# A Mamba-2 and MLA trunk on one core: sums of squares of weights drawn beneath the next projections, stores of converted pairs held back by one load, the first scan in two parts

## Chip, core and metric

The kernel runs on one core of a Trainium2 chip. Its time is the device time of one execution in microseconds (us). A core has a matrix engine (TensorE, PE in the profile), a vector engine (VectorE, DVE), a scalar engine (ScalarE, ACT) and GpSimd (POOL); all of the loads and stores that matter here are issued by SyncE (SP) in one queue. Each engine works through its own instructions in order and waits for others by semaphores.

## The reference

Two layers over 2048 tokens of width 1024, float32. The change lies in the first, a Mamba-2 mixer:

```python
proj = h @ w_in                                  # 1024 -> z 2048, xBC 2048 + 2*4*128, dt 32
z, xBC, dt_raw = jnp.split(proj, [D_INNER, D_INNER + CONV_DIM], axis=-1)
xBC = jax.nn.silu(causal_depthwise_conv(xBC, conv_w, conv_b))
xs, Bm, Cm = jnp.split(xBC, [D_INNER, D_INNER + SSM_GROUPS * SSM_STATE], axis=-1)
dt = jax.nn.softplus((dt_raw + dt_bias).astype(jnp.float32))
y = ssd_chunked_scan(xh, dt, A, Bm, Cm)          # 4 groups of 8 heads of 64, state 128
y = (y + D_skip[:, None] * xh).reshape(Bsz, S, D_INNER) * jax.nn.silu(z)
y = y * lax.rsqrt(jnp.mean(y * y, axis=-1, keepdims=True) + EPS)   # by group
return (y * g_out) @ w_out                       # 2048 -> 1024
```

The second layer is multi-head latent attention (16 heads, 2048 tokens, causal), with a down-projected query and a shared latent key and value, and a final RMS norm follows.

## The kernel before

**Arithmetic.** A float32 product is made of three half-precision ones: each operand is split into a high and a low part (fp16 pairs, or fp32r halves), and `mm3` (L84 to L88) issues high by high, high by low and low by high into one PSUM bank. A weight that is split into an fp16 pair (`pair16`, L117 on ScalarE for the high part, L118 on VectorE for the low one) is first scaled by a power of two, so that its values lie in the range of fp16. That power comes from the weight's sum of squares: `scan` (L164) loads a group's weights tile by tile (L175), squares them on ScalarE with an accumulated sum (L180), adds the sums on VectorE (L183, L185), and `powers` (L140) sums over the partitions with a small matmul (L144) and makes the two powers, `up` and `down`, with eight small VectorE operations.

**Tiling.** The tokens go in 4 blocks of 512 (index b), the channels of the Mamba layer in 4 groups (g). One item is one (b, g). An item's work has four parts:

- `xbc` and `zgate` (L476, L509): the input projections of a group, 24 steps. The weights have three kinds: 0 is the columns of B and C (256 wide), 1 those of x (512), 2 those of the gate z (512). They come from `wpair` (L193). In block 0 it loads raw weights (L206, 3 buffers `wraw`), converts two k-slices into a `wsp` buffer (6 of them) and stores the pair to DRAM (`wi_d`, L209); in later blocks the pair is just loaded back (L211). The evacuations of xbc do the convolution (L494 to L503), those of zgate the gate (`sz`, L523, L524).
- `ssd` (L629): the chunked scan over the item's 512 tokens, cut into 20 pieces. It loads a broadcast of the cumulated decays (`big`, L662, from `cumT`), makes products of B and C (L665, L666), transposes x (L681), and runs a chain over VectorE, ScalarE, GpSimd and PE (L674 to L676, L684, L688, L696, L697, halves at L645 and L646, L702, L713, L718, L720, L723).
- `outp` (L530): the output projection of the item before, 8 steps; in block 0 its weights are loaded, split and stored too (L130, L109 to L113, `wo_d` at L551).
- At some items extra parts: for (0,0) and (0,1) the scan of group g + 2 (11 steps), for (1,0) `head_scale` (L407, 22 steps: 21 pieces of the later weights are loaded, L420, and squared, L421), for g = 2 the loading, normalizing and steps of the next block.

**The order of the work.** `mamba` (L313) makes one item after the other. For item n it lines up the parts: outp of item n − 1, xbc and zgate of item n + 1, then the extra ones. It counts their steps (`total`) and, while it goes through them one after the other, draws a piece of the item's own ssd each time that `done * total < 20 * step`. So the pieces are spread evenly over all the steps, the extra ones too. A scheduler then orders each engine's instructions by program order, as they become possible, with weight loads and their conversions moved ahead by `AHEAD` = 10. In front of the items stand the scan of group 0 by kinds (kind 0 by itself, then 1 and 2 together, the tiles kept in `held` so that they need no second load), `prep` (the norm and the transposes of the first tokens), `steps` (dt and its cumulated sums, L573 and L613 to L625), xbc and zgate of (0,0), and beside both of these the scan of group 1.

## Time and profile before

| | |
|---|---|
| median of 3 runs | 3186.62 us (3184.37 to 3187.11) |
| the profiled execution | 3185.83 us |
| its span in the trace | 3184.1 us |
| its mean granted clock of PE | 0.993 |
| PE busy | 3059.6 us, 96% of the span |
| VectorE, ScalarE busy | 2394.7 us (75%), 1929.9 us (61%) |
| DMA | 454.75 MB, mean 143 GB/s |

Busy time is the time during which an engine has an instruction under way. Stretches of the span are quoted as start:end, length, then the busy time and number of instructions of each engine in the stretch, the granted PE clock, the share of time in which the DMA engines were busy, and GB/s. A row of waits names who waited for what, for how long in total, how often, and the longest. A row of the timeline has the start in us, the length, and at the end in brackets how long the engine stood idle before it and for whom.

### The profile page before, as it was taken

The numbers are of one execution on the slowest core, as the hardware profiler recorded it, in microseconds if no ns is written. First come the engines' busy times: TensorE is split into PE (matmuls) and PEld (weight loads), VectorE is DVE, ScalarE is ACT, GpSimd is POOL, SyncE is SP. The second block draws the span as 40 slices with busy tenths as digits, with TensorE's granted clock in tenths as the row PEclk, the third lists the DMA queues.
The fourth block names the chain that finished last, engine by engine and source line by source line (L and its number), as shares of the span: only waits on it lengthen the run. The fifth ranks groups of instructions, "written<-read, shape, count | busy, mean of one in ns | idle before, by whom it ended". The sixth has DMA issues, their size and how long they took to land.

```text
span 3184.1 us, 51344 instructions
## 1 busy us (share of the span) xinstructions
PE 3059.6 (96%) x17746; PEld 2046.3 (64%) x17746; DVE 2394.7 (75%) x5191; ACT 1929.9 (61%) x4859; POOL 610.5 (19%) x842
## 2 busy tenths in 40 slices
PE   6999999899999999999999999999999999999998
PEld 3455555566556666655788888866666666666677
DVE  7778885677776776776967766668888888888665
ACT  8667554554544444455646554568888888888522
POOL 0212121121222111221211211222212222222100
PEclk9999999999999999999999999999999999999999
DMA  8667645433354344433565555632222322233484
GB/s 289 227 214 229 228 146 195 156 126 127 132 180 133 120 147 153 146 133 108 173 216 185 187 163 171 189 90 51 61 54 55 66 52 65 53 73 88 104 273 157
DMA packets 196586, 454.75 MB, mean 143 GB/s; under 512 B 29107, under 2 KB 52403, under 8 KB 194885
## 3 DMA queue, kind: packets, MB, share of 16 engines
q1 hardware_dynamic: 168468, 373.58, 36.0%
q0 software_dynamic: 27856, 77.89, 9.5%
q8 instruction: 140, 2.29, 0.3%
q14 instruction: 122, 0.99, 0.1%
HBM read 340.60 MB, written 110.76 MB: 142 GB/s over the span
## 4 chain that ended last, share of the span: by engine, by line
PE 64%; DVE 13%; ACT 8%; DMA 6%; issue 6%; POOL 1%; SPq 1%; ACTq 0%; DVEq 0%; POOLq 0%
PE mm L86 13%; PE mm L87 12%; PE mm L88 12%; PE tr L1081 6%; PE tr L87 4%; PE tr L86 4%; PE tr L88 3%; PE tr L1092 3%; PE tr L1091 3%; DVE cacc L500 3%; ACT Pr L1066 2%; DMA big<-cumT 2%; DMA wraw<-in_ssm_w_in_dram 1%; DVE PTs L118 1%; DVE big L674 1%
## 5 line engine op out<-in xcount | busy, mean ns | idle before, releaser
L118 DVE SCALAR_TENSOR_TENSOR PTs<-tr,PTs 128x512 f16<-128x512 f32 (+3 forms) x640 | 373.9, 605 | 77.0 <-ACT PTs L117 69.9
L1066 ACT ACTIVATE Pr<-mm,nm 128x512 f32<-128x512 f32 (+2 forms) x631 | 394.1, 635 | 49.3 <-DVE nm L1058 44.8
L1054 DVE TENSOR_REDUCE mx<-mm 128x1 f32<-128x512 f32 (+2 forms) x631 | 372.6, 602 | 32.4 <-PE mm L88 29.6
L117 ACT ACTIVATE PTs<-tr 128x512 f16<-128x512 f32 (+3 forms) x640 | 329.3, 544 | 99.5 <-PE tr L1081 97.6
L1081 PE MATMUL tr<-pack,Pr 128*128 128x128 f32 x2176 | 317.4, 273 | 1.8 <-ACT Os L1098 1.4
L86 PE MATMUL mm<-xT,wsp 128*128 128x512 f16 (+1 forms) x800 | 304.7, 381 | 0.1
L88 PE MATMUL mm<-xT,wsp 128*128 128x512 f16 (+1 forms) x800 | 303.3, 380 | 1.3 <-DVE wsp L118 1.2
L87 PE MATMUL mm<-xT,wsp 128*128 128x512 f16 (+1 forms) x800 | 303.7, 380 | 0.0
L1081 PEld LDWEIGHTS tr<-pack,Pr 128*128 128x128 f32 x2176 | 253.2, 141 | 69.1 <-ACT Os L1098 2.2
L688 ACT ACTIVATE Xw<-tr,d_wend 128x64 f32<-128x64 f32 x512 | 183.0, 358 | 133.8 <-DVE Xd L684 132.3
L86 PE MATMUL mm<-K,xT 96*128 96x512 f16 (+2 forms) x639 | 222.8, 349 | 27.2 <-ACT Pr L1066 23.7
L500 DVE SCALAR_TENSOR_TENSOR cacc<-craw,pack,cacc 128x512 f32<-128x512 f32 x288 | 213.3, 763 | 29.6 <-ACT cacc L498 28.0
L86 PE MATMUL mm<-wsp,xT 128*128 128x512 f16 (+1 forms) x640 | 232.5, 363 | 1.8 <-ACT craw L494 1.6
L87 PE MATMUL mm<-wsp,xT 128*128 128x512 f16 (+1 forms) x640 | 231.8, 362 | 0.0
L88 PE MATMUL mm<-wsp,xT 128*128 128x512 f16 (+1 forms) x640 | 231.2, 362 | 0.0
L88 PE MATMUL mm<-K,xT 96*128 96x512 f16 (+2 forms) x639 | 222.5, 348 | 0.0
L87 PE MATMUL mm<-K,xT 96*128 96x512 f16 (+2 forms) x639 | 221.7, 347 | 0.0
L1091 PE MATMUL tr<-PTs,xT 128*128 128x512 f16 (+3 forms) x640 | 221.3, 347 | 0.1
L86 PE MATMUL mm<-wsp,yT 128*128 128x512 f32 x512 | 208.4, 410 | 11.9 <-DVE sz L524 6.3
L646 POOL TENSOR_TENSOR Xp<-Xw,Xp 128x512 fp32r<-128x512 f32 x64 | 81.8, 1278 | 717.7 <-ACT Xp L645 389.6
L1092 PE MATMUL tr<-PTs,xT 128*128 128x512 f16 (+3 forms) x640 | 219.4, 347 | 0.0
L87 PEld LDWEIGHTS <-xT 96*128 96x128 f16 (+1 forms) x1152 | 112.7, 98 | 153.7 <-issue 65.0
(431 smaller groups left out, 7341.8 us busy)
## 6 DMA issues: line engine op xcount, KB each, us to landing
wsp<-wi_d SPq DMA_DIRECT2D x96, 512.0 KB, 3.7
wsp<-wo_d SPq DMA_DIRECT2D x96, 512.0 KB, 3.4
big<-cumT SPq DMA_DIRECT2D x64, 512.0 KB, 4.9
wi_d<-wsp SPq DMA_DIRECT2D x32, 512.0 KB, 3.5
wo_d<-wsp SPq DMA_DIRECT2D x64, 256.0 KB, 2.4
hx<-in_ssm_w_in_dram SPq DMA_DIRECT2D x48, 256.0 KB, 4.5
wraw<-in_ssm_w_in_dram SPq DMA_DIRECT2D x48, 256.0 KB, 3.7
wsp<-wi_d SPq DMA_DIRECT2D x48, 256.0 KB, 2.7
```

The source lines that it names most:

```text
L86: mm(out, l_hi, r_hi, start=start, stop=False)
L87: mm(out, l_hi, r_lo, start=False, stop=False)
L88: mm(out, l_lo, r_hi, start=False, stop=stop)
L117: self.nc.scalar.activation(hi, src, AF.Copy, scale=scale)
L118: self.nc.vector.scalar_tensor_tensor(lo, src, scale, hi, ALU.mult, ALU.subtract)
L500: nc.vector.scalar_tensor_tensor(acc, raw[:, k:k + TB], wk[k], acc, ALU.mult, ALU.add)
L688: act(Xw[:, hc], px[:, hc], AF.Copy, scale=wend[:, h0 + h:h0 + h + 1])
L1054: v.tensor_reduce(mx[:, n:n + 1], s[:, :w], AX.X, ALU.max)
L1066: nc.scalar.activation(x[:, :w], s[:, :w], AF.Exp, bias=nm, accum_out=sm[:, n:n + 1])
L1081: nc.tensor.transpose(pt[:, j * P:(j + 1) * P], st["P"][j][kb], self.ident)
L1091: nc.tensor.matmul(st["O"][:, c], vals[h][:, kb, :], u[:, 0], start=kb == 0, stop=False)
L1092: nc.tensor.matmul(st["O"][:, c], vals[h][:, kb, :], u[:, 1], start=False, stop=kb == nk - 1)
```

## The change

There are three edits.

1. **Scan and head scale beneath the projections.** The scan of group g + 2 and the head scale are no longer parts of their own. `beneath(part, other)` goes through xbc and zgate of the next item and takes one step of the scan after each of their steps, and only what is left over comes after them. `total` counts the projection steps alone, so the 20 ssd pieces are spread over these. The scan gets an argument `early`: with 2, three tiles' loads are issued before the first square. Head scale loads its raw pieces three deep in the same way.
2. **Stores after the next loads.** `wpair` and `outp` don't issue the store of a converted pair; they put it in `self.owed`, and `settle()` issues it after the raw loads of the next pair or unit (in blocks past the first, before the load of the pair).
3. **The first scans.** Group 0's kinds 1 and 2 are scanned apart: kind 1 ahead of `steps`, kind 2 beside xbc(0,0). Group 1's scan goes beside zgate(0,0) alone.

```diff
+    def wunit(self, src, n, scale=None, late=False, then=None):
...
             self.nc.sync.dma_start(raw[:, :n], src)
+            if then:
+                then()
...
+    def scan(self, g, kinds, place, hold=False, early=0):
...
+        ready = []
+        for m, (kind, i, per) in enumerate(todo):
+            while len(ready) < min(m + 1 + early, len(todo)):
+                ready.append(fetch(*todo[len(ready)]))
+            junk = self.t(self.sp, "yt", [P, D], BF16, bufs=2)
+            nc.scalar.activation(junk, ready[m], AF.Square, accum_out=ss[:, kind, i:i + 1])
...
+    def settle(self):
+
+        for d, u in self.owed:
+            self.nc.sync.dma_start(d, u)
+        self.owed = []
...
+                self.settle()
+                for j, raw in enumerate(raws):
                     self.pair16(u[:, j, 0], u[:, j, 1], raw, self.up[:, g, kind:kind + 1])
-                nc.sync.dma_start(d, u)
+                self.owed.append((d, u))
             else:
+                self.settle()
                 nc.sync.dma_start(u, d)
...
+        def beneath(part, other):
+            for _ in part:
+                next(other, None)
+                yield
...
-        rest = self.scan(0, (1, 2), lambda kind: first.pop(0), True)
+        rest = [self.scan(0, (kind,), lambda kind: first.pop(0), True) for kind in (1, 2)]
         ahead = self.scan(1, (0, 1, 2), later)
-        for part in (hold, self.prep(0, self.g0), rest, self.steps(0), together(self.xbc(0, 0), ahead),
+        for part in (hold, self.prep(0, self.g0), rest[0], self.steps(0), together(self.xbc(0, 0), rest[1]),
                      together(self.zgate(0, 0), ahead)):
...
-                parts += [self.xbc(*items[n + 1]), self.zgate(*items[n + 1])]
+                beside = iter(())
+                if b == 0 and g < 2:
+                    beside = self.scan(g + 2, (0, 1, 2), later, early=2)
+                elif b == 1 and g == 0:
+                    beside = self.head_scale()
+                parts += [beneath(self.xbc(*items[n + 1]), beside), beneath(self.zgate(*items[n + 1]), beside), beside]
...
-            if b == 0 and g < 2:
-                parts.append(self.scan(g + 2, (0, 1, 2), later))
-                total += 11
-            if b == 1 and g == 0:
-                parts.append(self.head_scale())
-                total += 22
```

What moves is seen best in the engines' orders of instructions. First ScalarE near the start, after the transposes of the first tokens (`xT`); `hs` and `yT` hold the raw weights of kinds 1 and 2 of group 0, `big` those of kind 0, and `wsp<-` is a conversion. Before:

```order
L180 ACTIVATE yt_318,ss_307<-hs_209 128x1024
L117 ACTIVATE xT_304<-tr_299,pack 128x512
L180 ACTIVATE yt_322,ss_307<-hs_210 128x1024
L180 ACTIVATE yt_327,ss_307<-yT_211 128x1024
L180 ACTIVATE yt_331,ss_307<-yT_212 128x1024
L180 ACTIVATE yt_335,ss_307<-yT_213 128x1024
L180 ACTIVATE yt_339,ss_307<-yT_214 128x1024
L117 ACTIVATE wsp_428<-big_205,up 128x256
```

And after (the changed file's own line numbers: L187 is the square, L601 belongs to `steps`):

```order
L187 ACTIVATE yt_318,ss_307<-hs_209 128x1024
L117 ACTIVATE xT_304<-tr_299,pack 128x512
L187 ACTIVATE yt_322,ss_307<-hs_210 128x1024
L117 ACTIVATE wsp_410<-big_205,up 128x256
L117 ACTIVATE wsp_436<-big_205,up 128x256 x2
L117 ACTIVATE wsp_463<-big_206,up 128x256 x2
L117 ACTIVATE wsp_496<-big_206,up 128x256 x2
L117 ACTIVATE wsp_542<-hs_207,up 128x512 x2
L601 ACTIVATE yt_357<-tr_339,dtdown 64x512
L187 ACTIVATE yt_424,ss_421<-yT_211 128x1024
```

The four squares of kind 2 stand behind nine conversions and the first operation of `steps`.

Next PE where zgate(0,0) ends and xbc(0,1) begins; the first rows are the last products of zgate, `wsp_907` (before) and `wsp_921` (after) are the first pair of group 1. Before:

```order
L88 LDWEIGHTS xT_304
L88 MATMUL mm_772<-wsp_863,xT_304 128x512
L86 LDWEIGHTS wsp_907
L86 MATMUL mm_905<-xT_248,wsp_907 128x512
L87 LDWEIGHTS wsp_907
L87 MATMUL mm_905<-xT_248,wsp_907 128x512
```

After (L146 is the powers' matmul, L689 to L705 are the first of ssd(0,0)):

```order
L88 LDWEIGHTS xT_304
L88 MATMUL mm_713<-wsp_841,xT_304 128x512
L146 MATMUL tr_904<-ss_732,ones 128x3
L689 MATMUL tr_956<-pack,BC_517 128x128
L690 MATMUL tr_956<-BC_535,BC_517 128x128
L705 MATMUL tr_986<-pack,xs_653 128x128
L705 MATMUL tr_986<-pack,xs_671 128x128
L705 MATMUL tr_986<-pack,xs_689 128x128
L705 MATMUL tr_986<-pack,xs_707 128x128
L86 LDWEIGHTS wsp_921
L86 MATMUL mm_919<-xT_248,wsp_921 128x512
```

The matmul that ends group 1's scan, which stood within xbc(0,0) before, has come to the end of zgate(0,0), directly in front of the products that use its powers; six small matmuls stand between.

Last SP's queue at the same place; `wraw` are raw weights of group 1, `hx` tiles of a scan, `big` the decays, `hs` tokens of x. Before, from the second raw load on:

```order
L206 DMA wraw_912<-in_ssm_w_in_dram 128x2x128
L206 DMA wraw_976<-in_ssm_w_in_dram 128x2x128
L175 DMA hx_1628<-in_ssm_w_in_dram 128x2x128
L662 DMA big_924<-cumT_424 128x1024
L209 DMA wi_d<-wsp_691 128x2048
L662 DMA big_1132<-cumT_424 128x1024
L209 DMA wi_d<-wsp_773 128x2048
L209 DMA wi_d<-wsp_803 128x2048
L209 DMA wi_d<-wsp_833 128x2048
L209 DMA wi_d<-wsp_863 128x2048
L175 DMA hx_1628<-in_ssm_w_in_dram 128x2x128
L206 DMA wraw_980<-in_ssm_w_in_dram 128x2x128
```

After, two pieces of the same stretch (L221 is the raw load, L176 a scan tile's, L204 a store, L686 the decays, L561 x), first from the second raw load to behind the third:

```order
L221 DMA wraw_924<-in_ssm_w_in_dram 128x2x128
L204 DMA wi_d<-wsp_841 128x2048
L176 DMA hx_938<-in_ssm_w_in_dram 128x2x128 x4
L176 DMA hx_943<-in_ssm_w_in_dram 128x2x128 x4
L176 DMA hx_948<-in_ssm_w_in_dram 128x512 x2
L686 DMA big_954<-cumT_406 128x1024
L176 DMA hx_980<-in_ssm_w_in_dram 128x512 x2
L221 DMA wraw_1012<-in_ssm_w_in_dram 128x2x128
L176 DMA hx_1027<-in_ssm_w_in_dram 128x512 x2
```

Four more tiles (hx_1059 to hx_1145) follow, and then:

```order
L176 DMA hx_1145<-in_ssm_w_in_dram 128x512 x2
L686 DMA big_1150<-cumT_406 128x1024
L561 DMA hs_1844<-in_x_dram 128x1024
L561 DMA hs_1845<-in_x_dram 128x1024
L561 DMA hs_1846<-in_x_dram 128x1024
L561 DMA hs_1847<-in_x_dram 128x1024
L221 DMA wraw_1014<-in_ssm_w_in_dram 128x2x128
L204 DMA wi_d<-wsp_921 128x1024
```

Nine tiles of group 2's scan and the four loads of x have come in front of group 1's fourth raw weight, and the stores of its pairs behind the raw loads that follow.

More of the change, by code (lines that the diff above doesn't have):

```diff
@@ L124, in raw @@
         return self.t(self.sp, self.raws[0], [P, TB], bufs=2)
-    def wunit(self, src, n, scale=None, late=False):
+    def wunit(self, src, n, scale=None, late=False, then=None):
         with self.tc.high_priority(AHEAD):
@@ L162, in w_in, with fetch @@
         return w[:, c0:c0 + 512]
-    def scan(self, g, kinds, place, hold=False):
+    def scan(self, g, kinds, place, hold=False, early=0):
         nc = self.nc
         ss = self.t(self.sm, "ss", [P, 3, 4], bufs=2)
-        for kind in kinds:
-            per = 4 if kind == 0 else 2
-            for i in range(KD // per):
-                x = place(kind)
-                n = D // per
-                for j in range(per):
-                    d = x[:, j * n:(j + 1) * n]
-                    nc.sync.dma_start(d.rearrange("p (n c) -> p n c", n=2) if kind == 0 else d,
-                                      self.w_in(kind, g, per * i + j))
-                    if hold:
-                        self.held[kind, g, per * i + j] = d
-                junk = self.t(self.sp, "yt", [P, D], BF16, bufs=2)
-                nc.scalar.activation(junk, x, AF.Square, accum_out=ss[:, kind, i:i + 1])
-                yield
-            if kind == 0:
-                nc.vector.tensor_tensor(ss[:, 0, 0:1], ss[:, 0, 0:1], ss[:, 0, 1:2], ALU.add)
-            else:
-                nc.vector.tensor_reduce(ss[:, kind, 0:1], ss[:, kind, :], AX.X, ALU.add)
+        todo = [(kind, i, 4 if kind == 0 else 2) for kind in kinds for i in range(2 if kind == 0 else 4)]
+        def fetch(kind, i, per):
+            x, n = place(kind), D // per
+            for j in range(per):
+                d = x[:, j * n:(j + 1) * n]
+                nc.sync.dma_start(d.rearrange("p (n c) -> p n c", n=2) if kind == 0 else d,
+                                  self.w_in(kind, g, per * i + j))
+                if hold:
+                    self.held[kind, g, per * i + j] = d
+            return x
+        ready = []
[4 more added lines that the diff above has]
+            nc.scalar.activation(junk, ready[m], AF.Square, accum_out=ss[:, kind, i:i + 1])
+            if i == KD // per - 1:
+                if kind == 0:
+                    nc.vector.tensor_tensor(ss[:, 0, 0:1], ss[:, 0, 0:1], ss[:, 0, 1:2], ALU.add)
+                else:
+                    nc.vector.tensor_reduce(ss[:, kind, 0:1], ss[:, kind, :], AX.X, ALU.add)
+            yield
         lo, hi = kinds[0], kinds[-1] + 1
@@ L201, in wpair @@
             if b == 0:
+                raws = []
                 for j in range(2):
@@ L207, in wpair @@
                                           self.w_in(kind, g, k + j))
+                    raws.append(raw)
+                self.settle()
+                for j, raw in enumerate(raws):
                     self.pair16(u[:, j, 0], u[:, j, 1], raw, self.up[:, g, kind:kind + 1])
-                nc.sync.dma_start(d, u)
+                self.owed.append((d, u))
             else:
+                self.settle()
                 nc.sync.dma_start(u, d)
@@ L319, in mamba @@
         self.layer_constants(cp)
-        self.held = {}
+        self.held, self.owed = {}, []
         first = [self.t(self.sp, "big", [P, D], bufs=2) for _ in range(2)]
@@ L330, in together @@
                 yield
+        def beneath(part, other):
+            for _ in part:
+                next(other, None)
+                yield
         hold = self.scan(0, (0,), lambda kind: first.pop(0), True)
-        rest = self.scan(0, (1, 2), lambda kind: first.pop(0), True)
+        rest = [self.scan(0, (kind,), lambda kind: first.pop(0), True) for kind in (1, 2)]
         ahead = self.scan(1, (0, 1, 2), later)
-        for part in (hold, self.prep(0, self.g0), rest, self.steps(0), together(self.xbc(0, 0), ahead),
+        for part in (hold, self.prep(0, self.g0), rest[0], self.steps(0), together(self.xbc(0, 0), rest[1]),
                      together(self.zgate(0, 0), ahead)):
@@ L415, in head_scale @@
         pieces += [(1, a["kv_w_down"][k * P:(k + 1) * P, 256:288], self.gk[:, k:k + 1]) for k in range(KD)]
-        at = [0, 0, 0]
-        for i, src, gain in pieces:
-            n = src.shape[1]
-            raw = self.t(self.wp, "wraw", [P, TB], bufs=WRAW)
-            nc.sync.dma_start(raw[:, :n], src)
+        at, raws = [0, 0, 0], []
+        for m, (i, src, gain) in enumerate(pieces):
+            while len(raws) < min(m + 3, len(pieces)):
+                raws.append(self.t(self.wp, "wraw", [P, TB], bufs=WRAW))
+                ahead = pieces[len(raws) - 1][1]
+                nc.sync.dma_start(raws[-1][:, :ahead.shape[1]], ahead)
+            raw, n = raws[m], src.shape[1]
             nc.scalar.activation(self.t(self.sp, "yt", [P, D], BF16, bufs=2)[:, :n], raw[:, :n], AF.Square,
@@ L548, in weights @@
                 w = self.wunit(a["ssm_w_out"][r0:r0 + P, n * 512:(n + 1) * 512], 512,
-                               self.go[:, 4 * g + j:4 * g + j + 1])
-                for i in range(2):
-                    nc.sync.dma_start(d[:, i], w[i].bitcast(F32))
+                               self.go[:, 4 * g + j:4 * g + j + 1], then=self.settle)
+                self.owed += [(d[:, i], w[i].bitcast(F32)) for i in range(2)]
                 return w
```

## The prediction

> **What bounds the kernel now.** I read the page first, then the waits of TensorE, then the busy times of stretches cut at the ends of the items. The page says that TensorE (PE) is the engine to look at:

> ```profile
> span 3184.1 us, 51344 instructions
> PE 3059.6 (96%) x17746; PEld 2046.3 (64%) x17746; DVE 2394.7 (75%) x5191; ACT 1929.9 (61%) x4859; POOL 610.5 (19%) x842
> PE   6999999899999999999999999999999999999998
> ```

> PE idles 3184.1 − 3059.6 = 124.5 us. The profiled execution took 3185.83 us, 0.8 under the median of 3186.62; the sum is made against it. The change touches the program from its start to the end of item (1,0), the first 594 us, so the stretches go that far. Columns are start:end and length, then busy us (instructions) of PE, weight load, DVE, ACT and POOL, then the granted clock, the DMA share and GB/s:

> ```profile
> 60.00:100.00 40.00, 39.86 (x216) 18.85 (x215) 29.75 (x65) 24.55 (x54) 4.36 (x10) 1.00 0.89 294
> 90.00:158.00 68.00, 66.50 (x400) 34.24 (x398) 55.12 (x97) 47.40 (x115) 16.51 (x19) 1.00 0.66 213
> 158.00:190.00 32.00, 25.21 (x146) 19.07 (x146) 25.23 (x74) 26.01 (x70) 4.28 (x4) 0.84 0.85 261
> 190.00:254.00 64.00, 62.31 (x346) 32.94 (x345) 52.20 (x87) 39.89 (x90) 13.00 (x18) 1.00 0.58 185
> 254.00:294.00 40.00, 33.83 (x201) 23.81 (x200) 32.66 (x93) 33.65 (x84) 4.43 (x4) 0.96 0.86 283
> 294.00:354.00 60.00, 58.52 (x332) 30.53 (x331) 53.60 (x94) 41.33 (x95) 15.65 (x19) 1.00 0.62 199
> 458.00:478.00 20.00, 18.79 (x106) 11.28 (x102) 15.86 (x41) 9.18 (x19) 3.93 (x4) 1.00 0.50 171
> 478.00:558.00 80.00, 80.00 (x457) 46.43 (x456) 44.69 (x78) 34.85 (x93) 12.29 (x20) 1.00 0.57 196
> 558.00:594.00 36.00, 23.30 (x150) 17.34 (x149) 24.38 (x71) 25.72 (x88) 4.94 (x5) 0.81 0.55 169
> ```

> Item (0,0) is 90 to 190, (0,1) 190 to 294, (1,0) 478 to 594. While an item's projections run beside its SSD pieces, PE is 97 to 100% busy. When the projections are used up, only the scan of weights (or the head scale) is left to carry the remaining pieces, and PE falls to 79, 85 and 65%, twice at a lower clock. Item (0,3), with nothing of the kind, ends almost full (458 to 478). The waits of TensorE from 560 to 610, and three 4 us cuts of it, show what such a tail is made of:

> ```profile
> PE tr L723 <- DVE y L718: 5.4, 1, 5.4
> PE tr L86 <- ACT Xp L645: 3.1, 1, 3.1
> ```
> ```profile
> 574.00:578.00 4.00, 1.22 (x2) 0.50 (x2) 4.00 (x9) 2.97 (x10) 2.33 (x3) 0.50 0.09 15
> 578.00:582.00 4.00, 0.71 (x4) 0.71 (x4) 3.14 (x8) 1.75 (x4) 0.00 (x0) 0.50 0.05 8
> 582.00:586.00 4.00, 3.04 (x8) 2.11 (x7) 2.93 (x13) 2.61 (x12) 0.00 (x0) 0.50 0.45 131
> ```

> PE waits for links of the SSD chain (halves at L645, y at L718) with no projection to fill the wait.

> **The change part by part.**

> *First scan split by kind.* The waits of TensorE up to 60 us, its rows at 30.84, and ScalarE's rows ahead of that:

> ```profile
> PE tr L144 <- DVE ss L185: 7.0, 1, 7.0
> ```
> ```profile
> 30.84 0.56 PE L144 MATMUL tr<-ss,ones 128*128 128x2 f32 x2 [6.99 <-DVE ss L185]
> ```
> ```profile
> 26.25 1.06 ACT L180 ACTIVATE yt<-yT 128x1024 bf16<-128x1024 f32 x1
> ...
> 29.36 1.05 ACT L180 ACTIVATE yt<-yT 128x1024 bf16<-128x1024 f32 x1
> 30.40 2.89 ACT L117 ACTIVATE wsp<-big,up 128x256 f16<-128x256 f32 x7
> ```

> L144 waits 7.0 us for sums over both kinds. The four squares of kind 2 (yT) run from 26.25 to 30.40 and now come after L573 and the first conversions: 4.1 us gained, bounded by 0 and 4.1 (0 if they come back later on ScalarE's path). I take 4.1: in 60 to 100 PE is busy 39.86 of 40, and ScalarE 24.55, which covers them; without that cover they cost 4.1. The one extra powers step is a matmul (0.56 above is two) and eight tiny vector operations before the z gate needs them; the same cover, nothing.

> *Tails.* In after the 20 SSD pieces are spread over projection steps alone, so no tail is left. What goes is the tails' idle time: 32 − 25.21 = 6.8, 40 − 33.83 = 6.2, 36 − 23.30 = 12.7, together 25.7; and the lowered clock: (1 − 0.84) × 25.21 = 4.0, (1 − 0.96) × 33.83 = 1.4, and in (1,0) half of 1.22 + 0.71 + 3.04 = 2.5, together 7.9. (For 558 to 594 I don't use the mean of 0.81, which counts idle slices too; the mean for 158 to 190 may do so in part, so 4.0 may be 2 to 4.) [...]

> What replaces it: an item ends as (0,3) does, with 20 − 18.79 = 1.2 idle, three times 3.6 (bounds 0 and 3.6, for the dense stretch may hold that loss already). And the pieces get denser. Item (0,0) had 80.35 us of DVE in 100 (55.12 + 25.23), now in about 93, 86%; (0,1) 84.86 in 104, now in 98, 87%. Item (0,2), which had no scan, ran DVE at 53.60 of 60, 89%, with PE still at 97.5%. So DVE is no bound, but its margin is thin: bounds 0 and 13 (both tails' idle time returns inside the items), and I take 4, nearer to the row of 294 to 354 with its 1.5 us idle than to the tails. Item (1,0) has 69.07 of DVE in 116, now some 101: nothing.

> *Entry to (0,1)'s projections.* In before the second scan ran beside xbc(0,0) and the first pairs were converted long before PE needed them. In after its powers stand behind zgate(0,0) on PE, then come eight vector operations, ScalarE's conversion and DVE's rest. How long such a chain is shows at the start, where the same steps follow each other, on PE and on ScalarE:

> ```profile
> 16.37 0.59 PE L144 MATMUL tr<-ss,ones 128*128 128x1 f32 x2 [5.53 <-DVE ss L183]
> ```
> ```profile
> 18.13 0.51 ACT L117 ACTIVATE wsp<-big,up 128x256 f16<-128x256 f32 x1 [0.96 <-DVE up L152]
> ```

> From 16.37 to 18.13 + 0.51 is 2.3 us, and the vector part follows. PE has only the first small matmuls of the SSD (L665, L666, L681) to put there. Behind it raw weights refill three buffers at a time, with a landing time from the list of DMA issues (KB each, us to landing):

> ```profile
> wraw<-in_ssm_w_in_dram SPq DMA_DIRECT2D x48, 256.0 KB, 3.7
> hx<-in_ssm_w_in_dram SPq DMA_DIRECT2D x48, 256.0 KB, 4.5
> wi_d<-wsp SPq DMA_DIRECT2D x32, 512.0 KB, 3.5
> ```

> The lead that the six wsp buffers held has to be built up again. By the order, nine scan tiles (4.7 MB), two of cumT (1 MB) and four of x (2 MB) also stand between raw weights 2 and 4 on SP's queue, where before two of cumT, five stores and half a scan tile stood. At 294 GB/s (60 to 100) the extra 4 or 5 MB are about 15 us, spent while zgate(0,0) runs if squares free the hx buffers in time, after it if not. So: lower bound 1 us, upper 15, and I take 5, the chain and one late refill. [...]

> *Stores behind the next loads.* The waits of SP's queue over the first 600 us:

> ```profile
> SPq L209 <- DVE wsp L118: 66.5, 34, 12.5
> SPq L551 <- ACT wsp L112: 57.5, 21, 9.5
> ```

> In before a store at the queue's head waits up to 12.5 us for its conversion, and the next raw loads stand behind it. Now they pass it. ScalarE felt that, in waits of at most 2.4 us (the waits of all engines over the same time):

> ```profile
> ACT wsp L117 <- DMA wraw<-in_ssm_w_in_dram: 27.7, 21, 2.4
> ```

> PE, with pairs in hand, felt little of it, so 1 us, bounded by 0 and 2. A pair keeps its wsp buffer a little longer; six of them cover it. Head scale's loads run three deep, which only matters in its own, vanished tail.

> *Sum:* −4.1 − 25.7 − 7.9 + 3.6 + 4 + 5 − 1 = −26.1, so 3185.8 − 26.1 = 3159.7, or about 3160. Its bounds: with the best ends (handovers 0, pieces 0, entry 1, stores 2) 3147; with entry at 15, or with the pieces at 13, some 3169; with both 3179.

> **The rivals.**

> *In-order engines give it back.* Squares of 1.06 us now stand between evacuations on ScalarE, and more pieces per projection stand on DVE. If the two items of block 0 get nothing (their dense stretches at 87% DVE stretch by what the tails lose), the gain is the start 4.1, (1,0)'s 12.7 + 2.5 − 1.2, and the store's 1, less the entry's 5: 14.1, 3172. For it: 0.97 PE at 89% DVE is the best row there is; against: ScalarE has 73.4 busy in 100.

> *Slower: the one load queue.* All loads are on SP in order, and now 20 tiles of 512 KB go ahead of raw weights that PE is about to need. A tile lands in 4.5 us against 1.06 for its square; if PE waits the difference each time, 20 × 3.4 = 69, 3160 + 69 = 3229. It is slower than before once a tile costs PE over 26/20 = 1.3 us. Against it: (0,0) moves 68 × 0.213 + 32 × 0.261 = 22.8 MB, over 93 us 246 GB/s, under the 294 held for 40 us above. For it: the loads come bunched, early in each item. [...]

> *The idle time only moves.* If the tails are as long as they are because the SSD chain itself is that long (5.4 for one y), spreading the pieces shifts the waits to where the projections end: no change, 3186 within 6. Against it: (0,3) ends at 94% with the same pieces.

> **How the numbers follow.** The forecast, 3160 (own range 3147 to 3179), has 0.64: each tail ends in a wait that a projection would fill, and (0,2) and (0,3) show what items without a tail look like. In-order giving back 0.20 (3172, spread 3166 to 3179); the load queue 0.08; idle time that moves 0.08. The range 3147 to 3180 holds nearly all of the first two, 0.84. 0.2% is 6.4 us, about what a measurement of this kernel can tell from no change; faster is under 3180.2: 0.64 + 0.20 = 0.84; same 0.08; slower 0.08.

> **What would show it.** Right: L144's wait of 7.0 falls to about 3; no stretch of (0,0), (0,1) or (1,0) with PE under 90%; the clock at 1.00 there; items ending near 92 us after their start for (0,0), 97 for (0,1), 101 for (1,0). Wrong: PE waits over 10 us for L118 or L117 behind zgate(0,0) (entry), ScalarE's waits for wraw over 60 us (queue), DVE over 92% with PE under 95% in the two items (first rival), or waits for y L718 as long as before. Beyond 594 us nothing but the shift should differ.

## The result and the profile after

The changed kernel takes 3163.99 us (median of 6 runs, 3160.43 to 3165.87) against 3185.75 for before in the same session (3184.37 to 3190.44). The ratio is 0.9928, 95% interval 0.9915 to 0.9941: 22.9 us faster (18.8 to 27.1); the two medians alone differ by 21.8. The forecast was 3160, in a range from 3147 to 3180. The page after:

```profile
span 3162.4 us, 51356 instructions
PE 3052.1 (97%) x17748; PEld 2043.4 (65%) x17748; DVE 2396.4 (76%) x5200; ACT 1927.1 (61%) x4859; POOL 604.5 (19%) x842
PE   7899999999999999999999999999999999999998
```

Idle time of PE fell from 124.5 to 110.3 us, and its busy time by 7.5, though it does two matmuls more: it runs less of them at a lowered clock (mean granted clock 0.996 after 0.993). To see where, I cut both traces where an item's output projection ends and the next projection starts. In before these points are 90.7, 197.3, 299.2, 404.7, 497.0 and 604.8; in after 89.7, 193.0, 294.4, 401.1, 493.5 and 584.4.

| stretch | before | after | difference |
|---|---|---|---|
| start to the first product of xbc(0,1) | 90.7 | 89.7 | −1.0 |
| from there to the end of outp(0,0) | 106.6 | 103.3 | −3.3 |
| to the end of outp(0,1) | 101.9 | 101.4 | −0.5 |
| to the end of outp(0,3) | 197.8 | 199.1 | +1.3 |
| to the end of outp(1,0) | 107.8 | 90.9 | −16.9 |
| the rest of the span | 2579.3 | 2578.0 | −1.3 |

Three quarters of the gain stand in one item, (1,0). The other rows lie within some 3 us, which is how well a stage's time repeats in two profiles of the same code (see the experiments). The stretches of after, cut at its own stages (projections, then output projection):

```profile
60.00:85.00 25.00, 25.00 (x118) 11.29 (x117) 14.54 (x32) 17.77 (x32) 3.40 (x10) 1.00 1.00 322
85.00:93.00 8.00, 4.57 (x20) 2.27 (x19) 7.00 (x24) 6.44 (x23) 0.00 (x0) 0.79 0.54 205
93.00:168.00 75.00, 66.35 (x422) 34.21 (x421) 64.67 (x131) 53.87 (x130) 15.63 (x22) 1.00 0.67 216
168.00:193.00 25.00, 25.00 (x143) 20.24 (x142) 18.39 (x41) 17.93 (x43) 2.57 (x2) 1.00 0.79 259
193.00:268.00 75.00, 67.63 (x392) 35.99 (x392) 64.79 (x140) 55.89 (x132) 14.13 (x20) 0.95 0.71 235
268.00:294.00 26.00, 25.11 (x139) 19.90 (x138) 22.76 (x51) 14.67 (x37) 2.60 (x2) 1.00 0.67 220
493.00:558.00 65.00, 64.00 (x390) 33.27 (x390) 48.40 (x111) 43.85 (x127) 15.58 (x21) 1.00 0.66 226
558.00:584.00 26.00, 26.00 (x148) 21.09 (x147) 15.59 (x29) 8.24 (x26) 3.04 (x3) 1.00 0.39 122
```

The output projections, which held the tails, are now full (25.00 of 25, 25.11 of 26, 26.00 of 26). In (1,0) the projections are full too, 64.00 of 65. In block 0 they are not: 66.35 and 67.63 of 75, where the dense stretches of before were at 97%. So PE still idles as long in these two items, and now inside the projections. From the first product of xbc(0,1) to the end of outp(0,1), first before and then after:

```profile
90.70:299.20 208.50, 192.48 (x1108) 113.90 (x1108) 169.68 (x356) 148.19 (x360) 39.51 (x46) 0.97 0.70 223
```
```profile
89.70:294.40 204.70, 187.75 (x1101) 111.97 (x1102) 173.49 (x365) 145.66 (x353) 34.93 (x46) 0.98 0.70 227
```

Idle is 16.0 before and 17.0 after; the 3.8 us gained are busy time (192.5 to 187.8), of which PE ran 13.7 us at half clock before and 9.8 after. That part isn't the change's: a kernel whose code in this stretch is that of before (head scale alone, below) took 206.3 us in its profile, with 17.5 idle and 3.4 at half clock:

```profile
90.40:296.70 206.30, 188.81 (x1109) 110.55 (x1108) 169.55 (x356) 148.15 (x360) 39.72 (x46) 0.99 0.69 224
```

What PE waits for in the stretch, before:

```profile
PE mm L86 <- DVE sz L524: 3.3, 3, 1.6
PE tr L696 <- DVE big L676: 2.9, 2, 1.8
PE mm L86 <- DVE hs L559: 2.9, 2, 2.3
```

and after, from 90.6 to 294.4, where L720 is L696 and L700 is L676 (the first product's wait of 3.4 us ends at 89.73 and belongs to the entry, shown further down):

```profile
PE tr L720 <- DVE big L700: 5.8, 2, 3.1
PE mm L86 <- ACT wsp L117: 2.6, 2, 1.3
PE mm L87 <- DVE wsp L118: 1.7, 1, 1.7
```

The waits for the gate and the residual (`sz`, `hs`), with which a tail begins, gave way to longer waits for links of the SSD chain in the middle of the projections, and to some 5 us of waits for weights that are not converted yet. ScalarE ahead of one of the latter (PE's product waits until 219.25) has three squares of the scan among evacuations, and then the conversion:

```profile
213.26 1.05 ACT L187 ACTIVATE yt<-hx 128x1024 bf16<-128x1024 f32 x1
...
215.00 1.05 ACT L187 ACTIVATE yt<-hx 128x1024 bf16<-128x1024 f32 x1
...
216.72 1.05 ACT L187 ACTIVATE yt<-hx 128x1024 bf16<-128x1024 f32 x1
...
218.49 1.32 ACT L117 ACTIVATE wsp<-wraw,up 128x512 f16<-128x512 f32 x2
```

The start did as forecast. L146 (L144 in before) waits for the sum of kind 1 alone, in the waits up to 60 us:

```profile
PE tr L146 <- DVE ss L192: 2.8, 1, 2.8
```

instead of 7.0, and zgate(0,0) ends at 85.2 instead of 90.5, 5.3 earlier. Most of that is spent at the entry to xbc(0,1):

```profile
85.70 0.60 PE L705 MATMUL tr<-pack,xs 128*128 128x128 f32 x4
89.73 0.61 PE L86 MATMUL mm<-xT,wsp 128*128 128x512 f16 x1 [3.44 <-ACT wsp L117]
90.14 0.63 PE L87 MATMUL mm<-xT,wsp 128*128 128x512 f16 x1
...
92.27 0.62 PE L88 MATMUL mm<-xT,wsp 128*128 128x512 f16 x1
92.70 0.41 PE L87 MATMUL mm<-xT,wsp 128*128 128x512 f16 x1
92.94 0.38 PE L88 MATMUL mm<-xT,wsp 128*128 128x512 f16 x1
```

The last row before the gap ends at 86.30, the next product starts at 89.73, and the first seven come 0.43 us apart instead of 0.22: 3.4 + 1.5 = 4.9 us. VectorE's rows show why the chain is longer than at the start: from the first of the powers' operations to `up` it takes 2.1 us, with operations of the SSD and the gate between them:

```profile
86.76 0.15 DVE L148 TENSOR_SCALAR pwx<-tr 128x3 f32<-128x3 f32 x1
...
87.64 0.68 DVE L708 TENSOR_TENSOR Xd<-tr,d_dt 128x512 f32<-128x512 f32 x1
88.24 0.68 DVE L549 SCALAR_TENSOR_TENSOR sz<-sz,mm 128x512 f32<-128x512 f32 x1
88.83 0.16 DVE L154 TENSOR_SCALAR up<-pw 128x3 int32<-128x3 int32 x1
```

### The profile page after: what moved, and what is told of

Its sections match the earlier page's. It is cut to its first block, busy times and chain, and to the rows that moved or that the text cites. A ratio compares the mean times of both kernels' runs of the same rounds, so it can differ in the third digit from the quotient of the medians.

```text
span 3162.4 us, 51356 instructions
## 1 busy us (share of the span) xinstructions
PE 3052.1 (97%) x17748; PEld 2043.4 (65%) x17748; DVE 2396.4 (76%) x5200; ACT 1927.1 (61%) x4859; POOL 604.5 (19%) x842
## 4 chain that ended last, share of the span: by engine, by line
PE 61%; DVE 12%; ACT 7%; issue 5%; DMA 4%; POOL 1%; SPq 0%; ACTq 0%; DVEq 0%; POOLq 0%
PE mm L86 12%; PE mm L87 12%; PE mm L88 12%; PE tr L1105 6%; PE tr L87 3%; PE tr L86 3%; PE tr L88 3%; PE tr L1115 3%; PE tr L1116 3%; DVE cacc L525 3%; ACT Pr L1090 2%; DMA big<-cumT 2%; DVE PTs L118 1%; DVE big L698 1%; PE tr L720 1%
## 5 line engine op out<-in xcount | busy, mean ns | idle before, releaser
L118 DVE SCALAR_TENSOR_TENSOR PTs<-tr,PTs 128x512 f16<-128x512 f32 (+3 forms) x640 | 374.2, 606 | 76.3 <-ACT PTs L117 69.6
L117 ACT ACTIVATE PTs<-tr 128x512 f16<-128x512 f32 (+3 forms) x640 | 328.9, 543 | 99.7 <-PE tr L1105 97.8
L86 PE MATMUL mm<-xT,wsp 128*128 128x512 f16 (+1 forms) x800 | 305.5, 382 | 6.0 <-ACT wsp L117 6.0
L86 PE MATMUL mm<-K,xT 96*128 96x512 f16 (+2 forms) x639 | 222.6, 348 | 26.7 <-ACT Pr L1090 23.1
L86 PE MATMUL mm<-wsp,xT 128*128 128x512 f16 (+1 forms) x640 | 231.4, 363 | 1.7 <-ACT craw L519 1.7
L86 PE MATMUL mm<-wsp,yT 128*128 128x512 f32 x512 | 206.4, 405 | 3.5 <-DVE sz L549 1.0
## 6 DMA issues: line engine op xcount, KB each, us to landing
wsp<-wi_d SPq DMA_DIRECT2D x96, 512.0 KB, 3.6
wsp<-wo_d SPq DMA_DIRECT2D x96, 512.0 KB, 3.4
big<-cumT SPq DMA_DIRECT2D x64, 512.0 KB, 4.9
wi_d<-wsp SPq DMA_DIRECT2D x32, 512.0 KB, 3.6
wo_d<-wsp SPq DMA_DIRECT2D x64, 256.0 KB, 2.7
hx<-in_ssm_w_in_dram SPq DMA_DIRECT2D x48, 256.0 KB, 4.5
wraw<-in_ssm_w_in_dram SPq DMA_DIRECT2D x48, 256.0 KB, 3.7
wsp<-wi_d SPq DMA_DIRECT2D x48, 256.0 KB, 2.7
```

Of the source, the lines that this page charges most:

```text
L86: mm(out, l_hi, r_hi, start=start, stop=False)
L117: self.nc.scalar.activation(hi, src, AF.Copy, scale=scale)
L118: self.nc.vector.scalar_tensor_tensor(lo, src, scale, hi, ALU.mult, ALU.subtract)
```

## The experiments

Theory A, formed from the two traces: in (1,0) the gain is real; in block 0 the idle time of the tails came back inside the projections. Its rivals were the prediction's own terms. The changed kernel itself was timed in the first session alone, so its 22.9 is set beside the others by way of their kernels before. All ratios below are to the kernel before in the same session, with 95% intervals, and the us are that ratio times its median there (3182.0, 3183.0 and 3184.6 in the three sessions). Stage times come from one profile each, and repeat only within some 3 us: the head scale run below, whose code is the same as before's up to (1,0), reached the end of outp(0,0) 2.7 us earlier.

**Head scale beneath, alone.** The kernel before, with this and with the raw pieces loaded three deep as in the change

```diff
-                parts += [self.xbc(*items[n + 1]), self.zgate(*items[n + 1])]
+                beside = self.head_scale() if b == 1 and g == 0 else iter(())
+                parts += [beneath(self.xbc(*items[n + 1]), beside), beneath(self.zgate(*items[n + 1]), beside), beside]
...
-            if b == 1 and g == 0:
-                parts.append(self.head_scale())
-                total += 22
```

> The kernel before with one part of the change alone: head scale beneath xbc and zgate of (1,1), its loads three deep, no steps of its own. Theory A (in block 0 the idle time of the tails came back inside the projections, in (1,0) it did not): nearly the whole of the change's gain, 15 to 17 us off, about 3169. The prediction's own terms for (1,0) give 12.7 + 2.5 - 1.2 = 14, 3172. Rival: if (1,0) gains only because stores or scans moved as well, less than 8 us.

Measured: 3167.96 us, ratio 0.9953 (0.9942 to 0.9965), 15.0 us faster. Its item (1,0) takes 90.8 us, and PE has no idle time in the output projection:

```profile
495.00:560.00 65.00, 64.11 (x392) 33.35 (x391) 48.19 (x111) 44.15 (x127) 15.62 (x21) 1.00 0.65 222
560.00:586.00 26.00, 26.00 (x147) 21.07 (x146) 15.03 (x28) 8.11 (x25) 3.05 (x3) 1.00 0.37 122
```

These are the rows of the whole change. So (1,0)'s gain needs nothing else, and it is 15 (11 to 19) of the 22.9. All the traces agree: from the end of outp(0,3) to that of outp(1,0) it takes 90.4 to 92.0 us in the nine kernels with head scale beneath, and 107.4 to 108.3 in the five without.

**Scans beneath, alone.** The kernel before, with the new `scan` and

```diff
+                beside = self.scan(g + 2, (0, 1, 2), later, early=2) if b == 0 and g < 2 else iter(())
+                parts += [beneath(self.xbc(*items[n + 1]), beside), beneath(self.zgate(*items[n + 1]), beside), beside]
...
-            if b == 0 and g < 2:
-                parts.append(self.scan(g + 2, (0, 1, 2), later))
-                total += 11
```

> The kernel before with the scans of groups 2 and 3 beneath the projections of (0,1) and (0,2), three tiles loaded ahead, nothing else. The prediction's terms: -13.0 of idle, -5.4 of clock, +2.4 of handovers, +4 for denser pieces, so 12 us off, about 3174. Theory A: the same time as before within 3 us, since PE waits inside the projections for SSD links and raw weights as long as it waited in the tails.

Measured: 3185.85 us, ratio 1.0014 (1.0005 to 1.0022), 4.5 us slower (1.6 to 7.0). The forecast's 12 us are refuted for this edit alone. Theory A's "within 3 us" is inside the interval, towards the slower side.

**First scans, alone.** The kernel before, with

```diff
-        rest = self.scan(0, (1, 2), lambda kind: first.pop(0), True)
+        rest = [self.scan(0, (kind,), lambda kind: first.pop(0), True) for kind in (1, 2)]
...
-        for part in (hold, self.prep(0, self.g0), rest, self.steps(0), together(self.xbc(0, 0), ahead),
+        for part in (hold, self.prep(0, self.g0), rest[0], self.steps(0), together(self.xbc(0, 0), rest[1]),
```

> The kernel before with the first scan split by kind and group 1's scan beside zgate(0,0) alone, nothing else. The prediction's terms: -4.1 at the start, +5 at the entry to xbc(0,1): within 2 us of before. Rival: the entry gap only costs what its wait shows (3.4 us), or less, and 2 to 5 us stay as gain.

Measured: 3188.09 us, ratio 1.0015 (1.0006 to 1.0024), 4.8 us slower (1.9 to 7.6). The first product of xbc(0,1) comes at 87.6, 3.1 earlier than before, but the end of outp(0,1) at 300.6, 1.4 later. The early start is lost in block 0. The execution in the trace took 3183.78 us, no longer than before's, so the trace doesn't hold the whole of the 4.8.

**Stores, alone.** The kernel before, with

```diff
+                self.settle()
+                for j, raw in enumerate(raws):
                     self.pair16(u[:, j, 0], u[:, j, 1], raw, self.up[:, g, kind:kind + 1])
-                nc.sync.dma_start(d, u)
+                self.owed.append((d, u))
...
```

> The kernel before with the stores of converted pairs issued behind the next loads, nothing else. The prediction's term: 1 us off (0 to 2). Rival: a pair's wsp buffer is held longer and the loads that now pass it bunch up, 2 to 4 us slower.

Measured: 3177.95 us, ratio 0.9987 (0.9979 to 0.9996), 4.1 us faster (1.3 to 6.7).

Together the four give −15.0 + 4.5 + 4.8 − 4.1 = −9.8, where the whole gives −22.9: the parts don't add. From the single intervals, the difference of 13.1 carries some 7 us to each side. The next three take one part out of the changed kernel each.

**All but the scans.**

```diff
-                if b == 0 and g < 2:
-                    beside = self.scan(g + 2, (0, 1, 2), later, early=2)
...
+            if b == 0 and g < 2:
+                parts.append(self.scan(g + 2, (0, 1, 2), later))
+                total += 11
```

> The changed kernel with the scans of groups 2 and 3 as parts of their own again, as before; head scale, stores and first scans stay changed. Alone, the four parts gave about -15 (head scale), +4.5 (scans), +4.8 (first scans), -4.1 (stores) against before: together -10, where the whole gave -22. If the parts simply add, this gives -14; if the missing -12 arise between the scans and another part, also -14; if they arise among the other three, -26. By the prediction's terms the scans bring 12, so this would give -10.

Measured: 3169.84 us, ratio 0.9960 (0.9948 to 0.9973), 12.7 us faster than before. So in the company of the others the scans beneath bring 22.9 − 12.7 = 10.2 us, where alone they cost 4.5. A difference of two such runs carries some 6 us to each side, here and in the next two.

**All but the stores.**

```diff
-                self.settle()
...
-                self.owed.append((d, u))
+                nc.sync.dma_start(d, u)
...
```

> The changed kernel with the stores issued at once again, as before. If the missing -12 arise between stores and scans (tiles and raw weights of a denser queue stand behind stores that wait for conversions), this gives about -6 against before; if elsewhere, about -18. By the prediction's term of 1 us it gives -21.

Measured: 3160.24 us, ratio 0.9930 (0.9918 to 0.9942), 22.3 us faster. The stores bring 0.6 in company, and the interaction isn't theirs: that would have left 6. Whether they bring 0.6 or the 4.1 that they gave alone, the intervals don't tell.

**All but the first scans.**

```diff
-        for part in (hold, self.prep(0, self.g0), rest[0], self.steps(0), together(self.xbc(0, 0), rest[1]),
+        for part in (hold, self.prep(0, self.g0), rest, self.steps(0), together(self.xbc(0, 0), ahead),
```

> The changed kernel with the first scans as before (kinds 1 and 2 together, group 1's beside xbc and zgate). If the first scans cost 4.8 as they did alone, this gives -27 against before; if the missing -12 arise between them and the scans, -14; by the prediction's terms (-4.1 and +5) -22.

Measured: 3164.55 us, ratio 0.9943 (0.9930 to 0.9956), 18.1 us faster. Head scale and stores alone make 19.1, so without the first scans' split the scans beneath are worth about −1 here, as they were worth −4.5 alone. With it they are worth 10.2. The two edits seem to help each other: the split costs 4.8 alone and 6.4 beside head scale and stores (19.1 to 12.7), and gains 4.8 where the scans run beneath (18.1 to 22.9). That gain by itself does not clear its 6 us; what does is the step of the scans from −4.5 alone to 10.2 in company, 14.7 with some 6 to each side.

The trace of the kernel with all but the scans shows what the split costs where the tails stay. In its waits from 88.2 to 301.9, first:

```profile
PE mm L88 <- DVE wsp L118: 4.4, 4, 1.6
PE tr L146 <- DVE ss L192: 3.8, 1, 3.8
PE tr L721 <- DVE big L701: 3.5, 2, 2.3
PE mm L86 <- ACT wsp L117: 3.0, 3, 1.5
PE mm L87 <- DVE wsp L118: 2.9, 1, 2.9
```
```profile
88.20:301.90 213.70, 189.60 (x1101) 111.07 (x1102) 173.19 (x363) 151.46 (x366) 38.76 (x46) 0.98 0.71 229
```

The two items take 213.7 us instead of 208.5. The weights lost their lead (4.4 + 3.0 + 2.9 = 10.3 us of waits for L117 and L118, 1.5 of them at the entry, before 88.2), and the tail's waits, with 3.8 for the scan's own sum, come on top. In the changed kernel waits for weights and for SSD links stand in the same stretch, and while PE waits for one the other makes progress. That reading fits the sums of idle time (24.1 here, 17.0 in after), but no run separates it.

**The entry gap.** The changed kernel, with

```diff
-together(self.xbc(0, 0), rest[1]),
+together(self.xbc(0, 0), rest[1], ahead),
```

> The changed kernel with group 1's scan drawn beside xbc(0,0) as well, so that its powers come before zgate(0,0) and the gap of 3.4 us at the entry to xbc(0,1), with its 7 matmuls at half clock (1.5 us), is gone: -26 to -27 against before if the gap is a cost of its own. If what waits there is raw weights or the SSD chain anyway, no change, -22.

Measured: ratio 0.9947 (0.9934 to 0.9961), 16.9 us faster than before; not better than the changed kernel's 22.9. The gap is gone, but much of its price has moved: xbc(0,0) takes 35.7 us instead of 32.2, with PE idle for 3.5 instead of 0.7 and ScalarE, which now has the squares there as well, busy for 34.24. This kernel's row, then that of the changed one:

```profile
32.60:68.30 35.70, 32.20 (x154) 14.62 (x154) 28.95 (x80) 34.24 (x65) 3.64 (x9) 1.00 0.93 311
```
```profile
32.40:64.60 32.20, 31.48 (x152) 14.67 (x152) 24.98 (x66) 31.48 (x60) 3.65 (x8) 1.00 0.87 297
```

The first product of xbc(0,1) comes at 88.9 against 89.7.

The last four ask what holds block 0 up: VectorE (V), ScalarE's squares (S), or raw weights (W), which have no run of their own. The first two leave out two of three taps in two items:

```diff
-                for k in range(1, 4):
+                for k in range(1, 2 if (b, g) in ((0, 1), (0, 2)) else 4):
```

> The kernel before, with two of the three VectorE taps of the convolution left out in xbc(0,1) and xbc(0,2) (the outputs of these are then another convolution's): 12 operations of 0.74 us, 8.9 us of VectorE, less in each of the items (0,0) and (0,1). The control for the next run. All theories: 0 to 6 us faster than before, since PE is 97% busy there and the taps are not in the tails.

Measured: 3176.24 us, ratio 0.9978 (0.9969 to 0.9987), 7.0 us faster.

> The changed kernel with the same taps left out. Theory V (block 0 gives little because VectorE, at 90 to 100% of the time there, makes PE wait for SSD links and pairs): (0,0) and (0,1) get shorter by 8 to 12 us in all, and the change's gain against the kernel with the same taps left out is 28 to 32 us instead of 22. Theory S (ScalarE's squares hold up the conversions) or W (raw weights come late): still about 22.

Measured: 3161.54 us, ratio 0.9929 (0.9916 to 0.9943), 22.6 us faster than before, that is 15.6 against the kernel with the same taps left out. In the stretch of the two items, first this kernel, then its control:

```profile
90.50:288.80 198.30, 187.63 (x1102) 110.44 (x1103) 157.23 (x341) 146.43 (x356) 32.93 (x46) 0.98 0.72 239
```
```profile
90.60:291.80 201.20, 185.60 (x1108) 111.17 (x1108) 153.06 (x327) 148.75 (x362) 33.21 (x46) 0.99 0.70 231
```

Theory V's 28 to 32 against the control are refuted by the 15.6: over the whole, the change is not worth more where VectorE is freer. In the stretch the traces are kinder to it. Relief on VectorE shortens it about as much in before (208.5 to 201.2) as in after (204.7 to 198.3), but in after it is PE's idle time that goes (17.0 to 10.7), in before that stays (16.0 to 15.6) and busy time goes, most of it time at half clock (13.7 to 3.4 us). So VectorE seems to hold PE up in the changed items, in part and by one profile each. That the whole changed kernel is no faster for it (22.6 against 22.9), though the stretch is shorter by 6.4 in the profile, stays open; in the same profile the next stretch, to the end of outp(0,3), takes 201.7 us against 199.1.

**Short squares.** The changed kernel, with

```diff
-            nc.scalar.activation(junk, ready[m], AF.Square, accum_out=ss[:, kind, i:i + 1])
+            c = 128 if early else D
+            nc.scalar.activation(junk[:, :c], ready[m][:, :c], AF.Square, accum_out=ss[:, kind, i:i + 1])
```

> The changed kernel with the squares of the scans of groups 2 and 3 taken over 128 of each tile's 1024 columns (their sums are then too small by that), all loads as they were: some 0.9 us less of ScalarE for each of 20 tiles, 18 us in all. Theory S: 6 to 10 us faster than the changed kernel, in (0,0) and (0,1). Theory V or W: within 2 us of it.

Measured: 3166.86 us, ratio 0.9944 (0.9931 to 0.9956), 17.8 us faster than before, so rather slower than the changed kernel than 6 to 10 faster. A short square takes 0.31 us in the trace, a whole one 1.05. Theory S falls, although the trace had shown squares in front of a conversion: taking that work away took no time away.

**Spread squares.** The changed kernel, with (`half` is true in block 0)

```diff
-            for _ in part:
-                next(other, None)
+            for n, _ in enumerate(part):
+                if n % 2 or not half:
+                    next(other, None)
```

> The changed kernel with a scan step beneath every second projection step of (0,1) and (0,2) instead of each, so that a scan's 10 squares and tile loads spread over the item instead of standing in its first half. Nothing is left out. Theory S or W: 3 to 5 us faster than the changed kernel, about -26 against before. Theory V: the same as it, -22 within 2.

Measured: 3161.46 us, ratio 0.9935 (0.9923 to 0.9948), 20.7 us faster: the same as the changed kernel, within the intervals. That the bunching of squares and tile loads costs 3 to 5 us isn't borne out; a smaller share isn't excluded, for in the trace the stretch of the two items takes 201.7 us instead of 204.7, with 14.4 idle.

## Why the prediction was right, and where it was not

- **The total.** 26.1 us were forecast and 22.9 measured; the time lies in the range. That it comes so near is in part luck: in the profiles the tails of block 0 fall short by 8.2, and (1,0) with 2.9 and the start and entry with 1.9 go beyond their terms. The range's upper end took two terms at their worst; with the start and the stores at 0 as well it would have been 3184. Of the signs of being right, L144's shorter wait and a full (1,0) came; a stretch with PE at 88% and one at a clock of 0.95 are against them.
- **Start.** "I take 4.1": 5.3 by the end of zgate(0,0).
- **Entry.** "I take 5": a gap of 3.4 and 1.5 of slow products. The 5 was for the chain and one late refill, with nothing for a lower clock; measured were a granted clock of 0.50 from 89.33 to 92.74 and seven products 0.43 us apart instead of 0.22. Up to the first product start and entry leave −1.0 where the sum had +0.9; the slow products stand behind it. The chain alone isn't the 3.4: the gap is 1.5 in the three kernels with the split in which scan steps stand beneath none of the projection steps or every second one (first scans alone, all but the scans, spread squares), and 2.6 to 4.4 in the four with a scan step beneath each. That this gap could be undone for itself is not borne out: without it xbc(0,0) takes 3.5 longer, and the whole was no faster.
- **Item (1,0).** Forecast −12.7 − 2.5 + 1.2 = −14.0, measured −16.9 in the profile and −15.0 by the run of this part alone. Shown.
- **The tails of block 0.** This step failed: "What goes is the tails' idle time", 6.8 + 6.2, and 5.4 of clock, less 6.4 of costs, in all −12.0. Measured −3.8 in the profile. The idle time is 17.0 us after 16.0 and, in the same code's second profile, 17.5; only the time at a lowered clock shrank, and that was 13.7 or 3.4 us in the two profiles of the same code, so part of the 5.4 was chance. By the runs, the whole less head scale's share is 22.9 − 15.0 = 7.9 (some 6 to each side), where the sum had 12.1 for the rest of the change, entry and stores included: that the idle time stayed is shown, how much of the 12.0 is lost with it is not. What I had read from (0,2), that 89% of VectorE leaves PE at 97.5%, doesn't hold for an item that also converts new weights and squares a scan: at 86% of VectorE (64.67 of 75) PE fell to 88%. So the first rival is what happened in these two items, if not by its mark (VectorE over 92%). Its total of 3172 was too high by what (1,0) and the start gave beyond their terms and by these 3.8.
- **Why they gave it back** is half known. Waits moved from the tails to SSD links and unconverted weights inside the projections, seen in the traces. Less VectorE work took 6.3 us of idle time out of the stretch, but neither that nor short nor spread squares made the whole kernel faster, so no single engine's load is shown to explain it. What may remain is the order: PE takes pieces and products in one fixed order, and stands behind each link that is late (5.8 us in two waits of L720 for L700). I have no run that changes only that.
- **Stores.** "1 us, bounded by 0 and 2": 4.1 alone, 0.6 in company; not settled between.
- **The load queue.** Refuted as a loss: the kernel is faster, DMA ran at 216 and 235 GB/s in the two items, and ScalarE's waits for raw weights, 27.7 us before, are 26.6.
- **Parts that don't add.** The sum treated start and tails as separate terms. The runs show that they aren't: the scans beneath lose 4.5 alone and bring 10.2 beside the other parts. That it is the split of the first scans that they need rests on differences of the size of their intervals.

ScalarE's waits over the first 600 us of the changed kernel, on which the load queue's verdict rests:

```profile
ACT wsp L117 <- DMA wraw<-in_ssm_w_in_dram: 26.6, 23, 2.9
```

## What to carry to other kernels

In (1,0) a tail in which the matrix engine waits for a long chain was won back by drawing the chain's pieces beneath dense products where the other engines have room (VectorE 64.0 of 91 us); in block 0, where they also convert weights for those products, waits as long came back in their midst. VectorE's busy share alone didn't foretell it: 89% of it left PE at 97.5% in (0,2), 86% at 88% in (0,0). Look at what the products themselves wait for before counting a tail's idle time as gain. And run the parts of a change alone and left out: here their sum was less than half of the whole, and one edit was worth −4.5 or +10 depending on another.

## What the hardware showed

In these traces a gap of PE cost more than its length where a stretch at half clock followed it. After 1.5 us (first scans alone, 86.09 to 87.60) the products follow 0.22 us apart at once. After the entry's 3.43 us they come 0.43 apart for 3.0 us, and in the changed kernel gaps of 3.15, 2.70 and 2.47 us (ending at 202.25, 253.35 and 365.69) did the same. The four stretches, at a granted clock of 0.50:

```profile
89.33:92.74 3.41, 3.00 (x8) 1.09 (x9) 2.81 (x8) 3.41 (x15) 0.00 (x0) 0.50 0.37 119
201.97:205.38 3.41, 3.13 (x35) 2.62 (x35) 1.31 (x3) 3.41 (x15) 0.19 (x1) 0.50 0.94 317
253.17:256.58 3.41, 3.23 (x35) 2.62 (x35) 3.32 (x6) 2.78 (x13) 1.32 (x2) 0.50 0.25 55
365.81:369.22 3.41, 3.41 (x15) 3.04 (x16) 2.90 (x5) 2.06 (x4) 0.00 (x0) 0.50 0.49 148
```

In before a gap of 2.31 us (181.58 to 183.89) did the same:

```profile
184.00:188.00 4.00, 4.00 (x11) 3.16 (x12) 3.86 (x7) 1.64 (x5) 1.70 (x2) 0.58 0.79 214
```

But the length alone doesn't decide it. The same 2.31 us at the same place in the head scale run (180.52 to 182.83), and 3.04 us in before (367.73 to 370.77), left the clock at 1.00. Here is what follows each of them:

```profile
183.00:187.00 4.00, 4.00 (x18) 3.27 (x19) 3.79 (x7) 1.43 (x4) 1.72 (x2) 1.00 0.82 228
```
```profile
371.00:375.00 4.00, 4.00 (x31) 3.48 (x30) 4.00 (x7) 3.78 (x7) 0.00 (x0) 1.00 0.27 96
```

The five gaps above that half clock followed, of 2.31 to 3.43 us, each left PE busy for 11 to 32% of such a slot. By the entry's 3.4 + 1.5, a wait of 3 us costs about 4.5 where it fills a slot so, and 3 where it doesn't, as an estimate.
